# Seven-product pairs in the first output block of a hybrid decoder layer, their shared products between the last gate tiles

## The chip, the cores and the metric

One core of one Trainium2 chip. The metric is the device time of one launch in microseconds (us); the kernel before takes 1085.87 us (median of 3 runs, 1085.77 to 1085.95). Engine names are those of the profile: PE is the matrix engine (PEld its weight loads), DVE the vector engine, ACT the scalar engine, POOL the general engine, SP the engine whose queue issues the loads.

## The reference

One decoder layer on 256 tokens of width 2048, all in float32. What the change touches is the output projection of the mixed heads:

```python
u = rmsnorm(h, ln1_w)
lru_x, lru_g, q, k, v, ret_g = split(u @ w_in)          # six pieces, 1024 columns each
y_lru = rg_lru(conv(lru_x)) * gelu(lru_g)               # (256, 1024)
y_ret = silu(ret_g) * group_norm(retention(q, k, v))    # (256, 1024)
h = h + concat([y_lru, y_ret]) @ w_out                  # (2048, 2048): the change is here
u = rmsnorm(h, ln2_w)
h = h + (silu(u @ w_ffn_gate) * (u @ w_ffn_up)) @ w_ffn_down
return rmsnorm(h, final_norm_w)
```

## The kernel before

**Precision.** Each float32 operand is cut in two parts that the PE takes at its fast rate: a high part, cast by ACT (L112), and a rest, subtracted by DVE (L113). A product of two such operands is three matmuls: high by high, high by low, low by high (`three`, L667 to L672). So each weight that is loaded costs ACT one cast and DVE one subtraction before PE can use it. A load is 128 partitions by 1024 columns (512 KB) into one of six `raw` tiles; its parts lie in one of four `wh` and one of four `wl` tiles. The loads run three ahead of their use.

**The order of the work.** A list named `program` holds the steps; each step names the weights it needs and the function that issues its matmuls. First come the six input projections. The last of them is `lru_gate`: eight tiles of 128 columns (`fm_tile`, L173 to L189, tiles named `fm`), each with 16 matmuls of 512 columns and 16 of 256 and two loads. After each, `lru_out` (L411) makes one piece of the left operand `y`: a copy and an add out of the accumulator, a multiply, a gelu by a square and a tanh, and a multiply with the recurrence `hs`. Two pieces make a pair `y[k]`, cut by `Left` (L537). `y[0]` to `y[3]` come from these tiles, `y[4]` to `y[7]` from the retention heads: `group_norm` (L510) scales the head outputs `o` (eight ACT operations and two of DVE per four heads), then `ret_y` (L525) turns each head by two PE transposes into a tile `yt`.

**Blocks.** Then come two output blocks and eleven of the feed-forward part, then the down projection. A block is 1024 columns by eight pairs of row tiles; its four accumulators are c11, c12, c21 and c22 (two token halves by two column halves). `room(index)` (L663) puts them in one of two sets of four PSUM banks: the even blocks in the set that `aux` uses, the odd ones in the set that `bank` uses, where the `fm` tiles are too. A *plain* pair is eight products, 24 matmuls of 512 columns (`plain`, L793), from two loads. A *summed* pair takes seven products by sums of its tiles, in two steps. Its *shared* step (`share`, L771) makes four products, 12 matmuls, into the four accumulators before the block begins. After a block's last shared step DVE and ACT combine the accumulators (L781 to L787). The *direct* step (`direct`, L789) later adds the other three products, 9 matmuls. For the shared step DVE adds weight tiles four times (L648, in `raw`) and the parts are cut in four pieces; for the direct step half of the weights is loaded and cut again. The left operand of such a pair needs four small sums (s1 to s4, L551 to L554) and their cut.

`SUMMED` (L32) names the summed pairs of each block, `STEPS` (L36) the order of plain steps (p), direct steps (d) and shared steps of the next block (s), and `PLAIN` (L35) the order of the plain pairs. Block 0 has no summed pair and holds two shared steps of block 1; block 1 has pairs 4 and 5.

**Queues.** Each engine works through its own queue in order. The order in each queue is set when the program is built, by a scheduler that keeps to the program's order but may put a later instruction ahead where it takes an earlier one not to be ready. `defer` and `tick` (L228 to L241) put off the heads' work by a number of steps.

Of the kernel before, what the change touches and what calls it, by code (L numbers as in the profile page):

```python
# [17 lines left out]
KT = D // P  # L18
DFF = 5632
FT = DFF // P  # L20
NLRU = 8
# [7 lines left out]

SUMMED = ((), (4, 5), (2, 3)) + ((1, 2, 3), (0, 1, 2, 3)) * 4 + ((1, 2, 3), (1, 2, 3))  # L32
SUMMED_OUT, SUMMED_FFN = (4, 5), (0, 1, 2, 3)

PLAIN = ((4, 5, 6, 7, 0, 1, 2, 3),) * 2 + (tuple(range(8)),) * 11  # L35
STEPS = ("pppspppspp", "ppspdpsdpp", "pdpsdpspspp") + ("pspsdpsdpsdp", "psdpsdpsddp") * 4 + ("psdpsdpsdpp", "psdpsdpsdpp")  # L36


EARLY_DOWN = (0, 1, 2)
# [5 lines left out]
def tile_hymba_layer(ctx: ExitStack, tc: tile.TileContext, A: dict, out: bass.AP):  # L45
# [33 lines left out]
    def bank(name):  # L79
        return pmm.tile([P, 512], F32, tag="mm", name=nm(name))  # L80

    def aux(name):
        return paux.tile([P, 512], F32, tag="aux", name=nm(name))
# [65 lines left out]
    program = []  # L149
# [23 lines left out]
    def fm_tile(unit, acts, order, post, room=bank):  # L173


        def run():
            ps = room("fm")
            for n in range(0, len(order), 2):
                if n == 8 and halfway:
                    halfway.pop()()  # L180

                two = [(*unit.part(k, P, 0, P), acts[k]) for k in order[n : n + 2]]
                for i, (wh, _, hl) in enumerate(two):
                    pe.matmul(ps, wh, hl, start=n + i == 0, stop=False)  # L184
                for i, (_, wl, hl) in enumerate(two):
                    pe.matmul(ps[:, :S], wl, hl[:, :S], start=False, stop=n + i == len(order) - 1)  # L186
            post(ps)

        program.append(([unit], run))  # L189
# [94 lines left out]
    u = [None] * KT  # L284
# [126 lines left out]
    def lru_out(n, ps):  # L411
        g, q = tmp("g"), tmp("q")
        halves(ps, g)
        v.tensor_tensor(out=g, in0=g, in1=r1, op=ALU.mult)
        act.activation(out=q, in_=g, func=AF.Square, scale=math.sqrt(0.044715))
        v.scalar_tensor_tensor(out=q, in0=q, scalar=1.0, in1=g, op0=ALU.add, op1=ALU.mult)
        act.activation(out=q, in_=q, func=AF.Tanh, scale=math.sqrt(2.0 / math.pi))
        v.scalar_tensor_tensor(out=g, in0=q, scalar=1.0, in1=g, op0=ALU.add, op1=ALU.mult)
        v.scalar_tensor_tensor(
            out=y_half(n), in0=g, scalar=0.5, in1=pair(hs, n, "hs"), op0=ALU.mult, op1=ALU.mult  # L420
        )
        y_done(n)

        cb, t = divmod(n, 2)
        htok[cb, t] = res_tile("htok")
        nc.sync.dma_start(out=htok[cb, t], in_=A["x_tok"][t * P : t * P + P, cb * 512 : cb * 512 + 512])
# [96 lines left out]
            v.tensor_scalar(out=gnh, in0=small[:, C_GN : C_GN + NH], scalar1=0.5, scalar2=None, op0=ALU.mult)  # L523

    def ret_y(h):  # L525
        ps = aux("yt")
        for t in range(2):
            o = oo[2 * t + h // 4][:, (h % 4) * P : (h % 4) * P + P]
            pe.transpose(ps[:, t * P : t * P + P], o, ident)
        act.activation(out=y_half(NLRU + h), in_=ps[:, :S], func=AF.Copy, scale=gnh[:, h : h + 1])  # L530
        y_done(NLRU + h)
# [527 lines left out]
        tm_block([Unit(A["w_rg"][4 * c + i]) for i in range(4)], lambda k: u[k], post)  # L1059
    head_at = len(program) - 8  # L1060

    for n in range(NLRU):
        fm_tile(Unit(A["w_lg"][n]), u, range(KT), lambda ps, n=n: lru_out(n, ps))

    def swap():

        early.close()
# [5 lines left out]
        for j in range(NB)  # L1073
    ]
    down = Block(NB + 2, lambda i: A["w_down"][i], dl, None, "", EARLY_DOWN, make_left)
    for b, after in zip(blocks, blocks[1:] + [down]):
        if b.index == 2:
            program.append(([], swap))
        b.put(after)
        if b.index == NB:  # L1080
            program.append(([], load_fw))
# [120 lines left out]
```

## Time and profile before

| | |
|---|---|
| median of 3 runs | 1085.87 us |
| profiled execution, first to last instruction | 1084.4 us |
| PE busy | 1074.2 us (99%) |
| DVE busy | 953.5 us (88%) |
| ACT busy | 660.9 us (61%) |
| mean granted PE clock | 0.999 |
| loads of weights, each 512 KB | 3.4 to 6.3 us from issue to landing |

The last input projection runs from 243.8 to 291.7 us after the start of the span, block 0 follows it. The profile gives a time to every instruction of each engine's queue, and for an idle stretch the engine that ended it. PE and DVE instructions overlap their neighbours, so the cost of one in a full queue is the distance from its start to the next start, and not the duration that its row lists.

### The profile page before, as it was taken

What the parts mean: (1) busy time and instruction counts of PE and PEld (TensorE: products, weight loads), DVE (VectorE), ACT (ScalarE), POOL (GpSimd) and SP (SyncE); (2) the same over time, 40 slices, a digit from 0 to 9 for tenths busy, and PEclk for the clock granted to TensorE, in tenths of its full rate; (3) what the DMA queues carried; (4) which work ended last, traced back from release to release, by engine and by line L of the source; (5) the groups of instructions that cost most, each with busy time, mean ns of one, the idle gap of its engine ahead of it and who ended that gap; (6) DMA issues with size and microseconds to landing.
All of it is one profiled execution on the core that took longest, in us unless ns stands there. A gap on an engine that the chain in (4) does not pass through costs nothing.

```text
span 1084.4 us, 14584 instructions
## 1 busy us (share of the span) xinstructions
PE 1074.2 (99%) x5101; PEld 899.5 (83%) x5101; DVE 953.5 (88%) x1371; ACT 660.9 (61%) x935; POOL 51.0 (5%) x61
## 2 busy tenths in 40 slices
PE   9999999999999999999999999999999999999997
PEld 7888888888888788888888888888888888888885
DVE  7789799988878889888998998999899899898986
ACT  7666644468746676565566566556556666655563
POOL 0612230000000000000000000000000000000001
PEclk9999999999999999999999999999999999999999
DMA  9964474444565567577677677686675756465652
GB/s 330 333 211 168 160 252 173 174 175 171 181 230 205 184 228 275 198 248 266 220 245 261 220 264 235 233 289 214 233 271 194 265 181 213 171 214 199 212 209 85
DMA packets 69274, 238.32 MB, mean 220 GB/s; under 512 B 7888, under 2 KB 8272, under 8 KB 69200
## 3 DMA queue, kind: packets, MB, share of 16 engines
q1 hardware_dynamic: 68400, 235.29, 62.7%
q0 software_dynamic: 512, 1.57, 0.4%
q8 instruction: 40, 0.66, 0.2%
q10 hardware_dynamic: 288, 0.52, 0.1%
q14 instruction: 34, 0.28, 0.1%
HBM read 235.26 MB, written 2.10 MB: 219 GB/s over the span
## 4 chain that ended last, share of the span: by engine, by line
PE 97%; DVE 1%; issue 1%; DMA 0%; ACT 0%; POOL 0%; SPq 0%; POOLq 0%; ACTq 0%
PE c L670 22%; PE c L672 22%; PE c L671 22%; PE fm L184 11%; PE fm L186 5%; PE tm L164 3%; PE tm L165 3%; PE tm L166 3%; PE p L672 1%; PE p L671 1%; PE p L670 1%; PE ft L833 1%; DMA raw<-in_w_v 0%; PE ht L576 0%; PE sc L482 0%
## 5 line engine op out<-in xcount | busy, mean ns | idle before, releaser
L112 ACT CAST wh<-raw 128x1024 fp32r<-128x1024 f32 (+1 forms) x490 | 460.9, 965 | 362.6 <-PE c L672 132.5
L113 DVE TENSOR_TENSOR wl<-raw,wh 128x1024 fp32r<-128x1024 f32 (+1 forms) x490 | 538.2, 1122 | 91.2 <-ACT wh L112 88.4
L671 PE MATMUL c<-wl,ah 128*128 128x512 f32 x850 | 331.0, 390 | 0.0
L672 PE MATMUL c<-wh,al 128*128 128x512 f32 x850 | 330.4, 389 | 0.0
L670 PE MATMUL c<-wh,ah 128*128 128x512 f32 x850 | 275.0, 391 | 0.2 <-ACT wh L112 0.2
L670 PEld LDWEIGHTS c<-wh,ah 128*128 128x128 f32 x850 | 159.4, 188 | 33.4 <-ACT wh L112 1.1
L672 PEld LDWEIGHTS c<-wh,al 128*128 128x128 f32 x850 | 159.6, 188 | 33.0
L671 PEld LDWEIGHTS c<-wl,ah 128*128 128x128 f32 x850 | 159.6, 188 | 32.7
L184 PE MATMUL fm<-u,wh 128*128 128x512 f32 x512 | 161.3, 396 | 0.0
L186 PEld LDWEIGHTS fm<-u,wl 128*128 128x128 f32 x512 | 96.0, 188 | 22.5
L186 PE MATMUL fm<-u,wl 128*128 128x256 f32 x512 | 101.1, 278 | 0.0
L184 PEld LDWEIGHTS fm<-u,wh 128*128 128x128 f32 x512 | 78.4, 189 | 0.3
L648 DVE TENSOR_TENSOR raw<-raw,raw 128x512 f32<-128x512 f32 x106 | 73.1, 690 | 2.8
L648 DVE TENSOR_TENSOR raw<-raw 128x512 f32<-128x512 f32 x106 | 72.7, 689 | 2.4
L671 PE MATMUL c<-wl,sh 128*128 128x512 f32 x176 | 68.5, 389 | 0.0
L672 PE MATMUL c<-wh,sl 128*128 128x512 f32 x176 | 68.0, 389 | 0.0
L670 PE MATMUL c<-wh,sh 128*128 128x512 f32 x176 | 60.4, 394 | 0.3 <-ACT sh L112 0.3
L165 PE MATMUL tm<-wl,u 128*128 128x512 f32 x128 | 48.8, 394 | 0.0
L166 PE MATMUL tm<-wh,u 128*128 128x512 f32 x128 | 48.7, 390 | 0.0
L164 PE MATMUL tm<-wh,u 128*128 128x512 f32 x128 | 47.3, 398 | 0.8 <-ACT u L288 0.8
L954 POOL TENSOR_TENSOR htok<-htok,fw 128x512 f32<-128x512 f32 x2 | 2.5, 1273 | 895.9 <-ACT junk L947 895.9
L670 PEld LDWEIGHTS c<-wh,sh 128*128 128x128 f32 x176 | 33.1, 188 | 7.3 <-ACT sh L112 0.7
(245 smaller groups left out, 1034.9 us busy)
## 6 DMA issues: line engine op xcount, KB each, us to landing
raw<-in_w_gu SPq DMA_DIRECT2D x212, 512.0 KB, 5.5
raw<-in_w_down SPq DMA_DIRECT2D x91, 512.0 KB, 4.3
raw<-in_w_out SPq DMA_DIRECT2D x34, 512.0 KB, 3.7
raw<-in_w_lx SPq DMA_DIRECT2D x16, 512.0 KB, 6.3
raw<-in_w_k SPq DMA_DIRECT2D x16, 512.0 KB, 3.5
raw<-in_w_q SPq DMA_DIRECT2D x16, 512.0 KB, 4.0
raw<-in_w_rg SPq DMA_DIRECT2D x16, 512.0 KB, 3.4
raw<-in_w_lg SPq DMA_DIRECT2D x16, 512.0 KB, 3.4
```

The costliest lines, as they stand in the source:

```text
L112: act.copy(out=dst_h, in_=src)
L113: v.tensor_tensor(out=dst_l, in0=src, in1=dst_h.bitcast(F32), op=ALU.subtract)
L164: pe.matmul(ps, ah, wh, start=first, stop=False)
L165: pe.matmul(ps, ah, wl, start=False, stop=False)
L166: pe.matmul(ps, al, wh, start=False, stop=last)
L184: pe.matmul(ps, wh, hl, start=n + i == 0, stop=False)
L186: pe.matmul(ps[:, :S], wl, hl[:, :S], start=False, stop=n + i == len(order) - 1)
L648: v.tensor_tensor(out=dst, in0=a, in1=b, op=ALU.add)
L670: pe.matmul(p, ah, bh, start=first, stop=False, skip_group_check=onto)
L671: pe.matmul(p, ah, bl, start=False, stop=False, skip_group_check=onto)
L672: pe.matmul(p, al, bh, start=False, stop=last, skip_group_check=onto)
L833: pe.transpose(pt[:, o : o + P], g[:, (2 * b + c) * P : (2 * b + c) * P + P], ident)
```

## The change

Block 0 takes pairs 4 and 5 as summed pairs, and block 1 takes pair 6 besides 4 and 5. Pair 6 (heads 4 and 5) gets the sums of its left tiles. The two shared steps of block 0 are put into `program` behind gate tiles 3 and 5 (counted from 0). Since the accumulators of block 0 then hold all four banks of the `aux` set from the first shared step on, the transposes of `ret_y` go to the other set. Block 0 holds three shared steps of block 1. The line numbers of the new kernel are 2 higher than those of the old up to L1060.

```diff
-SUMMED = ((), (4, 5), (2, 3)) + ((1, 2, 3), (0, 1, 2, 3)) * 4 + ((1, 2, 3), (1, 2, 3))
-SUMMED_OUT, SUMMED_FFN = (4, 5), (0, 1, 2, 3)
+SUMMED = ((4, 5), (4, 5, 6), (2, 3)) + ((1, 2, 3), (0, 1, 2, 3)) * 4 + ((1, 2, 3), (1, 2, 3))
+SUMMED_OUT, SUMMED_FFN = (4, 5, 6), (0, 1, 2, 3)
+
+SHARED_FIRST = (3, 5)
...
-STEPS = ("pppspppspp", "ppspdpsdpp", "pdpsdpspspp") + ("pspsdpsdpsdp", "psdpsdpsddp") * 4 + ("psdpsdpsdpp", "psdpsdpsdpp")
+STEPS = ("pspdpspdpsp", "pdpspdpsdp", "pdpsdpspspp") + ("pspsdpsdpsdp", "psdpsdpsddp") * 4 + ("psdpsdpsdpp", "psdpsdpsdpp")
...
     def ret_y(h):
-        ps = aux("yt")
+        ps = bank("yt")
...
-    for n in range(NLRU):
-        fm_tile(Unit(A["w_lg"][n]), u, range(KT), lambda ps, n=n: lru_out(n, ps))
-
     def swap():
...
     down = Block(NB + 2, lambda i: A["w_down"][i], dl, None, "", EARLY_DOWN, make_left)
+
+    for n in range(NLRU):
+        fm_tile(Unit(A["w_lg"][n]), u, range(KT), lambda ps, n=n: lru_out(n, ps))
+        if n in SHARED_FIRST:
+            m = SHARED_FIRST.index(n)
+            program.append(([blocks[0].shared[m]], lambda m=m: blocks[0].share(m)))
+
```

**ACT's queue around the first gate tile.** sh_515 is the cut of the sums of `y[4]`; rg and sg are the retention gate and its tanh for the last four heads; yf_533 is `y[5]` out of its transposes, ah_535 its high part; the wh tiles are high parts of gate weights (wh_547 for the first half of gate tile 2), fm_549 is gate tile 0. Before:

```order
L112 CAST sh_515_2612<-s_514_2607 128x512
L473 ACTIVATE rg_528_2657<-tm_474_2414,r1_tok_108 128x512
L474 ACT_TABLE_LOAD
L474 ACTIVATE sg_529_2658<-rg_528_2657 128x512
L473 ACTIVATE rg_530_2674<-tm_475_2415,r1_tok_108 128x512
L112 CAST wh_557_2792<-raw_556_2791 128x1024
L170 COPY g_550_2758<-fm_549_2725 128x256
L474 ACTIVATE sg_531_2675<-rg_530_2674 128x512
L530 ACTIVATE yf_533_2682<-yt_532_2679,gnh_117 128x256
L530 ACTIVATE yf_533_2682<-yt_534_2684,gnh_117 128x256
L112 CAST wh_560_2798<-raw_559_2797 128x1024
L112 CAST ah_535_2688<-yf_533_2682 128x512
```

The same place in the changed kernel:

```order
L114 CAST sh_515_2612<-s_514_2607 128x512
L475 ACTIVATE rg_528_2657<-tm_474_2414,r1_tok_108 128x512
L476 ACT_TABLE_LOAD
L476 ACTIVATE sg_529_2658<-rg_528_2657 128x512
L475 ACTIVATE rg_530_2674<-tm_475_2415,r1_tok_108 128x512
L476 ACTIVATE sg_531_2675<-rg_530_2674 128x512
L532 ACTIVATE yf_533_2682<-yt_532_2679,gnh_117 128x256
L532 ACTIVATE yf_533_2682<-yt_534_2684,gnh_117 128x256
L114 CAST ah_535_2688<-yf_533_2682 128x512
L114 CAST wh_547_2720<-raw_546_2719 128x1024
L114 CAST sh_538_2697<-s_537_2692 128x512
L499 COPY o_483_2478<-pv_540_2701 128x128
```

The heads' work, up to the cut of `y[5]`, now stands ahead of the cut of gate weights: wh_547 comes behind it, where before wh_547 was long done and two later tiles (wh_557, wh_560) stood among the heads' rows.

**DVE's queue at the end of the gate tiles.** fm_641 is the last gate tile of the kernel before. Its rows there, and the first weights of block 1's first shared step (wl_662, raw_660):

```order
L171 TENSOR_TENSOR g_642_3219<-fm_641_3186,g_642_3219 128x256
L419 SCALAR_TENSOR_TENSOR yf_633_3170<-g_631_3161,hs_479_2451 128x256
L414 TENSOR_TENSOR g_642_3219<-g_642_3219,r1_109 128x256
L113 TENSOR_TENSOR wl_652_3244<-raw_650_3241,wh_651_3243 128x1024
L416 SCALAR_TENSOR_TENSOR q_643_3220<-q_643_3220,g_642_3219 128x256
L113 TENSOR_TENSOR wl_659_3278<-raw_657_3275,wh_658_3277 128x1024
L418 SCALAR_TENSOR_TENSOR g_642_3219<-q_643_3220,g_642_3219 128x256
L419 SCALAR_TENSOR_TENSOR yf_633_3170<-g_642_3219,hs_479_2451 128x256
L113 TENSOR_TENSOR wl_662_3284<-raw_660_3281,wh_661_3283 128x512
L113 TENSOR_TENSOR al_645_3230<-yf_633_3170,ah_644_3229 128x512
```

In the changed kernel c11_612, c12_615, c22_613 and c21_614 are block 0's accumulators; L785 to L789 combine them after its second shared step; raw_673, wl_675 and wl_666 belong to block 1's first shared step (wl_666 is written twice; this is its second half), fm's last values are g_668:

```order
L785 TENSOR_TENSOR p_648_3198<-c12_615_3040,p1_647_3197 128x512
L115 TENSOR_TENSOR wl_675_3334<-raw_664_3270,wh_674_3333 128x1024
L418 SCALAR_TENSOR_TENSOR q_669_3310<-q_669_3310,g_668_3309 128x256
L650 TENSOR_TENSOR raw_673_3325<-raw_673_3325 128x512
L786 TENSOR_TENSOR q_649_3199<-p_648_3198,c22_613_3032 128x512
L421 SCALAR_TENSOR_TENSOR yf_659_3260<-g_657_3251,hs_479_2451 128x256
L115 TENSOR_TENSOR wl_666_3273<-raw_673_3325,wh_665_3272 128x512
L420 SCALAR_TENSOR_TENSOR g_668_3309<-q_669_3310,g_668_3309 128x256
L788 TENSOR_TENSOR c22_613_3032<-q_649_3199,c21_614_3036 128x512
L789 TENSOR_TENSOR c21_614_3036<-c21_614_3036,p_648_3198 128x512
L115 TENSOR_TENSOR wl_680_3344<-raw_678_3341,wh_679_3343 128x1024
```

The shared step of block 1 and the combining of block 0's accumulators now stand among the last gate tiles' own rows; before, weights of plain pairs (wl_652, wl_659) stood there, and the first shared step began behind them.

**PE's queue where block 0 begins.** Before, the last gate tile (fm_641) is followed by block 0's first plain pair:

```order
L186 MATMUL fm_641_3186<-u_43_303,wl_626_3118 128x256
L670 MATMUL c11_653_3247<-wh_628_3124,ah_512_2603 128x512
L671 MATMUL c11_653_3247<-wl_629_3125,ah_512_2603 128x512
L672 MATMUL c11_653_3247<-wh_628_3124,al_513_2604 128x512
L670 MATMUL c12_654_3251<-wh_628_3124,ah_512_2603 128x512
L671 MATMUL c12_654_3251<-wl_629_3125,ah_512_2603 128x512
```

In the changed kernel block 1's first shared step (c11_687, c22_688, c21_689, c12_690) comes right behind the last gate tile, mixed with block 0's first plain pair (c11_612, c12_615). Here is the end of that step, 16 matmuls behind the last gate tile:

```order
L673 MATMUL c21_689_3391<-wl_675_3334,sh_515_2612 128x512
L674 MATMUL c21_689_3391<-wh_674_3333,sl_516_2613 128x512
L672 MATMUL c11_612_3028<-wh_679_3343,ah_604_3012 128x512
L673 MATMUL c12_690_3395<-wl_666_3273,sh_515_2612 128x512
L674 MATMUL c12_690_3395<-wh_665_3272,sl_516_2613 128x512
L672 MATMUL c12_615_3040<-wh_654_3214,ah_582_2919 128x512
```

The shared step of block 1 has moved up from behind three plain pairs to the very start of block 0.

## The prediction

> **What bounds the kernel now.** I read the page's busy times and chain first, then what PE waited for.
>
> ```profile
> PE 1074.2 (99%) x5101; PEld 899.5 (83%) x5101; DVE 953.5 (88%) x1371; ACT 660.9 (61%) x935; POOL 51.0 (5%) x61
> PE 97%; DVE 1%; issue 1%; DMA 0%; ACT 0%; POOL 0%; SPq 0%; POOLq 0%; ACTq 0%
> PE warm L105 <- DVE eps_t L98: 1.1, 1, 1.1
> PE tm L164 <- ACT u L288: 0.8, 2, 0.5
> PE c L670 <- ACT wh L112: 0.2, 1, 0.2
> ```
>
> PE is the bound, and its queue is nearly never empty: its waits add up to a few us, most of them at the start. A matmul taken out is worth its full slot, as long as PE stays fed. But DVE is at 88% on average, so the question is whether it can feed PE where the change puts its work: between the gate tiles. The windows view has DVE there, and at the end of block 0 and in block 1 (length, busy us, instructions):
>
> ```profile
> 245.10:294.25 49.15, 43.68 (x88) 1.00 0.49 176
> 364.00:391.00 27.00, 25.45 (x36) 1.00 0.67 242
> ```
>
> Along the gate tiles DVE has 5.47 us free in 49.15. It is also ahead of PE, but not by much: the rest of block 0's first weights is subtracted at 284.84 and done at 286.1, and PE takes it at 291.96, right behind the first row of block 0 (291.72). That lead, 5.9 us, is about what four split tiles allow: three lie ahead of the one in use.
>
> **The prices.** PE's timeline, for the slots:
>
> ```profile
> 243.78 0.62 PE L184 MATMUL fm<-u,wh 128*128 128x512 f32 x2
> 247.27 0.39 PE L491 MATMUL pv<-v,sc 128*128 128x128 f32 x2
> 247.94 0.60 PE L482 MATMUL sc<-rope,rope 128*128 128x256 f32 x2
> 248.59 0.60 PE L529 MATMUL yt<-ident,o 128*128 128x128 f32 x4
> 248.95 0.72 PE L184 MATMUL fm<-u,wh 128*128 128x512 f32 x2
> 291.72 0.40 PE L670 MATMUL c<-wh,ah 128*128 128x512 f32 x1
> 308.73 0.62 PE L670 MATMUL c<-wh,sh 128*128 128x512 f32 x2
> ```
>
> From 291.72 to 308.73 stand 75 matmuls of 512 columns: 0.227 each. The first gate tile makes ten matmuls of each size from 243.78 to 247.27, so a tile (16 of each) is 5.58. Three attention matmuls are 0.67, four transposes 0.36.
>
> DVE's timeline, for the distances between starts in a full queue:
>
> ```profile
> 258.00 0.28 DVE L551 TENSOR_TENSOR s<-yf 128x128 f32<-128x128 f32 x1
> 258.20 0.28 DVE L553 TENSOR_TENSOR s<-yf 128x128 f32<-128x128 f32 x1
> 258.40 0.48 DVE L499 BATCH_NORM_STATS2 st<-o 128x6 f32<-128x128 f32 x2
> 267.69 1.22 DVE L113 TENSOR_TENSOR wl<-raw,wh 128x1024 fp32r<-128x1024 f32 x1
> 268.82 0.16 DVE L255 TENSOR_TENSOR gr<-rs,rs 128x8 f32<-128x8 f32 x1
> 271.05 0.41 DVE L171 TENSOR_TENSOR g<-fm,g 128x256 f32<-128x256 f32 x1
> 271.39 0.41 DVE L418 SCALAR_TENSOR_TENSOR g<-q,g 128x256 f32<-128x256 f32 x1
> 284.84 1.22 DVE L113 TENSOR_TENSOR wl<-raw,wh 128x1024 fp32r<-128x1024 f32 x1
> 300.79 0.69 DVE L113 TENSOR_TENSOR wl<-raw,wh 128x512 fp32r<-128x512 f32 x1 [0.27 <-ACT wh L112]
> 301.40 0.68 DVE L113 TENSOR_TENSOR al<-yf,ah 128x512 fp32r<-128x512 f32 x1
> 302.00 0.68 DVE L648 TENSOR_TENSOR raw<-raw 128x512 f32<-128x512 f32 x1
> 302.72 1.42 DVE L648 TENSOR_TENSOR raw<-raw,raw 128x512 f32<-128x512 f32 x2
> 304.17 0.69 DVE L648 TENSOR_TENSOR raw<-raw 128x512 f32<-128x512 f32 x1
> 304.78 1.82 DVE L113 TENSOR_TENSOR wl<-raw,wh 128x1024 fp32r<-128x1024 f32 x2
> 306.52 0.68 DVE L113 TENSOR_TENSOR t4l<-raw,t4h 128x512 fp32r<-128x512 f32 x1
> 307.12 1.22 DVE L113 TENSOR_TENSOR wl<-raw,wh 128x1024 fp32r<-128x1024 f32 x1
> ```
>
> 1024 columns cost 1.14, 512 cost 0.61, 256 cost 0.34, a small sum 0.20, the four weight sums 2.78 (0.695 each). The last eight rows are one shared step: 0.61, 2.78, then 1.74 and 0.60, together 5.73, and a cut of left tiles (0.60) in between.
>
> **The change part by part.** *Removed.* Three pairs become summed ones, each three matmuls fewer: 9 × 0.227 = 2.04 us of PE. With a full queue that is 1085.87 − 2.04 = 1083.83. The profiled execution's span, 1084.4, is 1.5 below the median; I take that difference as unchanged.
>
> *Added to DVE.* A summed pair costs 5.73 for its shared and 1.14 for its direct step, where a plain pair costs 2 × 1.14: 4.6 more, 13.8 for three. The sums of `y[6]` add 4 × 0.20 + 0.61 = 1.4, the combining of block 0 another 4 × 0.61 = 2.4. So DVE gets 17.6 us more while PE gets shorter.
>
> *Where it lands.* Two shared steps go between the gate tiles, and by DVE's queue the first one of block 1 lies there too, and the combining. I count DVE's queue of the changed kernel from the cut of `y[4]`'s left tile to the second half of wl_666, for which the 18th matmul behind the last gate tile waits: 120 instructions, of which 18 × 1.14 = 20.5, 24 × 0.61 = 14.6, 38 × 0.34 = 12.9, 12 weight sums × 0.695 = 8.3, 12 small sums × 0.20 = 2.4, 16 short ones (statistics at 0.20, the rest down to 0.08, one of 384 columns) 2.1: 61.0 us. The same prices over the 88 instructions of the quoted window give 42.6 where the window has 43.68, so the count is, if anything, 2.5% low.
>
> DVE can begin when `y[4]` is out and cast. ACT's timeline:
>
> ```profile
> 243.07 0.84 ACT L530 ACTIVATE yf<-yt,gnh 128x256 f32<-128x256 f32 x2 [0.44 <-PE yt L529]
> 244.98 0.62 ACT L112 CAST ah<-yf 128x512 fp32r<-128x512 f32 x1
> 249.61 0.68 ACT L473 ACTIVATE rg<-tm,r_tok 128x512 f32<-128x512 f32 x1
> 250.31 1.28 ACT L474 ACT_TABLE_LOAD   x1
> 251.60 0.63 ACT L474 ACTIVATE sg<-rg 128x512 f32<-128x512 f32 x1
> 261.20 1.28 ACT L248 ACT_TABLE_LOAD   x1
> 270.07 3.18 ACT L520 ACTIVATE o<-o,gm,gr 128x128 f32<-128x128 f32 x8
> ```
>
> The cast now follows yf at once: 243.07 + 0.84 + 0.62 = 244.5. DVE is through at 244.5 + 61.0 = 305.5 if it never waits.
>
> PE's side: the attention and transposes that stood inside the first gate tile (247.27 to 248.95) now stand ahead of it, so the tile starts at 243.78 + 1.68 = 245.46. To the matmul in question stand 8 tiles (44.6), 24 + 17 matmuls of 512 columns (the two shared steps, and what precedes it behind the last gate tile), 9.3, eight transposes 0.7 and three attention matmuls 0.7: 55.3 us, so PE is there at 300.8. It waits at least 305.5 − 300.8 = 4.7.
>
> *DVE's own waits.* By ACT's new order the heads' work stands first. Walking both queues with these durations, DVE waits 0.5 for the cast of `y[4]`'s sums, 1.25 and 0.5 for the two sg behind the table load, 0.6 for `y[5]`'s cast, 0.45 around two more table loads, and 0.55 and 0.95 for the eight o's (3.18 on ACT): 4.8. From the first shared step on ACT has less to do than DVE, and DVE has no more waits. The bounds are 0 and the 5.5 that DVE had free in the quoted window; I take 4.8, since each of these waits has its row. PE's wait: 4.7 + 4.8 = 9.5. It shows in pieces: 1.6 at the transposes ahead of gate tile 3 (they need o, done on DVE at 264.5 by the walk; PE is there at 245.46 + 3 × 5.58 + 0.67 = 262.9), 2.6 in the first shared step, the rest in block 1's first shared step.
>
> *After that.* Block 0 has three shared, two direct and six plain steps: 12 + 9 matmuls three and two times and 24 six times, 198 × 0.227 = 44.9 on PE, against 3 × 5.73 + 2 × 1.14 + 12 × 1.14 = 33.2 of cuts and sums on DVE and some 7 beside. DVE gets its lead back there. In block 1 I count by the same prices 39.4 on DVE against 40.1 on PE over the shared steps of block 2; a lead of up to 5.9 covers that. Cost: 0; with no lead, PE waits once for a cast and a cut, the cut 1.14 and the cast about the same, 2.3.
>
> *At nothing.* Three more loads of 512 KB: SP issues them three loads ahead, and the six raw tiles cover their landing. Without that cover one is a few us. The other bank set for `ret_y`: gate tile 3 takes over the bank of gate tile 1, whose values DVE has read by 262.6, before PE asks at 262.9; 0 to 0.5.
>
> Sum: 1085.87 − 2.04 + 9.5 = 1093.3 us.
>
> **The clock.** The first matmuls of the run, after PE had nothing real to do, are slow; the third row is the settled rate:
>
> ```profile
> 4.93 1.22 PE L164 MATMUL tm<-wh,u 128*128 128x512 f32 x2
> 5.95 0.82 PE L165 MATMUL tm<-wl,u 128*128 128x512 f32 x2
> 6.61 0.63 PE L166 MATMUL tm<-wh,u 128*128 128x512 f32 x2
> ```
>
> The two slow rows lose 0.78 us against the third. [...] No row of the kernel before shows a fall in mid-kernel, since PE has no gap there. [...]
>
> **The rivals.** *PE stays full* (the other side): DVE's free 5.47 us and its 5.9 us lead take up the added work, and the nine matmuls are gain. Place: the 18th matmul of block 0. It decides if DVE's 61.0 plus waits come to less than 300.8 − 244.5 = 56.3. For it: PE never waited before at DVE loads as high as 25.45 in 27. Against: even with no wait the count is 4.7 too long. 1083.83.
>
> *Only one wait counts*: the transposes' 1.6 us are paid, and in that time DVE catches up for good. 1085.87 − 2.04 + 1.6 = 1085.4. Against it: DVE's total does not shrink while PE waits.
>
> *The clock falls* in the gaps, at three places: 3 × 0.78 = 2.3 more, 1095.6. For it: gaps of 2 us and more close together.
>
> *The lead is gone in block 1* as well, where DVE and PE are level by my count: PE waits again for a cast and a cut, 2.3, 1095.6; with the 2.5% by which my count may be low (1.5 us) 1097.1. For it: DVE's 25.45 in 27 before the change. Against: block 0 has room for the lead to come back.
>
> **How the numbers follow.** Chances: the forecast 0.66, PE stays full 0.08, only one wait 0.06, the clock 0.12, the lead 0.08. Around the forecast the bounds of DVE's waits give 1088.6 (none) to 1094.0 (5.5). The range is 1086.5 to 1097.5: below, the first bound less 2 us for a count 3% high; above, the last rival and a little. It leaves out the first two rivals and a twentieth above. 0.2% is 2.2 us, about what a measurement of this kernel can tell from no change. A full PE queue gains 2.04, just inside it, so faster by over 0.2% needs that rival and a little more: 0.03. Within 0.2% (1083.7 to 1088.0): 0.11. Slower: 0.86.
>
> **What would show it.** Right: DVE without idle stretches from the first shared step to block 0; PE waiting for DVE or ACT at yt, at c22 and c12 of the shared steps, about 9 us in all between 262 and 315; the last gate tile ending at about 291.7 + 5.4 + 4.2 = 301.3. Wrong: waits of PE under 4 us there; DVE with idle time between gate tiles 4 and 7; new PE waits in later blocks, which my counts deny; a granted clock under 1 in this stretch.

## The result, and the profile after

The changed kernel takes 1096.26 us (median of 4 runs, 1093.96 to 1098.16) against 1085.91 us (4 runs, 1085.77 to 1086.44) of the kernel before on the same chip: ratio of the means 1.0094, 95% interval 1.0082 to 1.0106, so 10.2 us slower (the medians lie 10.35 apart). The profiled execution took 1095.59 us, its span is 1093.7 us against 1084.4: 9.3 more.

Busy times and the chain of the changed kernel:

```profile
PE 1075.3 (98%) x5092; PEld 898.3 (82%) x5092; DVE 967.4 (88%) x1401; ACT 667.5 (61%) x947; POOL 50.9 (5%) x61
PE 94%; DVE 2%; ACT 1%; issue 1%; DMA 1%; POOL 0%; SPq 0%; POOLq 0%; ACTq 0%; DVEq 0%
```

PE has its nine matmuls less and yet more busy time: in part by its clock (below), and in part because a row of 0.39 us, which lies under its neighbour after 0.23 in a full queue, counts whole in front of a gap. DVE and ACT now hold 3% of the chain together. What PE waited for:

```profile
PE fm L186 <- ACT rg L475: 2.8, 1, 2.8
PE c L672 <- ACT wh L114: 2.4, 4, 1.2
PE c L673 <- DVE wl L115: 2.0, 2, 1.4
PE c L672 <- ACT p L784: 1.4, 1, 1.4
```

None of these is in the profile of before, but for 0.2 us. The first is in front of the first gate tile. PE's timeline there:

```profile
245.45 0.38 PE L485 MATMUL sc<-rope,rope 128*128 128x128 f32 x2
248.68 1.22 PE L186 MATMUL fm<-u,wh 128*128 128x512 f32 x2 [2.85 <-ACT rg L475]
...
252.21 0.63 PE L186 MATMUL fm<-u,wh 128*128 128x512 f32 x2
...
252.91 0.63 PE L186 MATMUL fm<-u,wh 128*128 128x512 f32 x2
```

From 245.45 to 248.68 PE does 0.11 us of work: a gap of 3.12 us. The four banks of the `bank` set then hold the two tiles of the retention gate (`tm`) and the two tiles of transposes (`yt`) that the change has put there, and the gate tile waits until ACT has copied a `tm` out. ACT's rows say why that is late: the copy stands behind a cut that waits for DVE.

```profile
247.43 0.62 ACT L114 CAST sh<-s 128x512 fp32r<-128x512 f32 x1 [1.77 <-DVE s L556]
247.95 0.68 ACT L475 ACTIVATE rg<-tm,r_tok 128x512 f32<-128x512 f32 x1
```

Behind the gap the matmuls are slow. Three sets of four take 3.53 us from 248.68 to 252.21, where the set from 252.21 to 252.91 takes 0.70: 1.43 us lost. The windows view (length, then busy us of PE, PEld, DVE, ACT, POOL, then the granted clock):

```profile
245.00:248.40 3.40, 0.83 (x6) 0.59 (x4) 2.88 (x11) 1.63 (x5) 0.00 (x0) 0.97 0.49 175
248.40:251.80 3.40, 3.12 (x10) 2.69 (x11) 1.53 (x3) 3.34 (x6) 0.00 (x0) 0.53 0.20 80
251.80:255.20 3.40, 3.40 (x23) 3.07 (x22) 2.63 (x7) 2.63 (x6) 0.00 (x0) 1.00 0.00 0
```

The clock is halved for 3.4 us. In these 3.4 us, where PE is late already, DVE is busy for only 1.53 us: it waits for ACT as well, so it gains little on PE.

The later waits, PE's rows in the first shared step and behind the last gate tile:

```profile
277.67 0.50 PE L673 MATMUL c<-wl,sh 128*128 128x512 f32 x1 [1.41 <-DVE wl L115]
...
303.95 0.39 PE L674 MATMUL c<-wh,al 128*128 128x512 f32 x1
...
305.72 0.50 PE L672 MATMUL c<-wh,ah 128*128 128x512 f32 x1 [1.38 <-ACT p L784]
...
309.16 0.50 PE L673 MATMUL c<-wl,sh 128*128 128x512 f32 x1 [0.58 <-DVE wl L115]
...
311.53 0.50 PE L672 MATMUL c<-wh,ah 128*128 128x512 f32 x1 [1.18 <-ACT wh L114]
311.87 0.40 PE L673 MATMUL c<-wl,sh 128*128 128x512 f32 x1
```

By the distances between starts PE loses 1.57 us in the first shared step and 4.15 in four gaps from 303.95 to 311.53. The last of these four ends with ACT's cast of a plain pair's weights, which by the profile had itself waited for PE:

```profile
310.43 1.04 ACT L114 CAST wh<-raw 128x1024 fp32r<-128x1024 f32 x1 [0.54 <-PE c L674]
```

A last gap of 0.90 us stands in block 1, at 385. The sum: 3.12 + 1.43 + 1.57 + 4.15 + 0.90 = 11.17, less 2.04 for the nine matmuls, is 9.13 of the 9.3 us.

DVE, at the place where the prediction's ledger ends (the second half of wl_666):

```profile
310.86 0.72 DVE L115 TENSOR_TENSOR wl<-raw,wh 128x512 fp32r<-128x512 f32 x1
```

It is done 0.60 later, at 311.5; the ledger with DVE's own waits said 310.3. So DVE's queue ends when the cast above does, and the 18th matmul could not have gone earlier than 311.5 without that cast either. From 270 to 312 us DVE has no idle time. From 244.4, the cut of `y[4]`, to 311.5 it waits for 6.4 us and works for 60.7.

### The profile page after: what moved, and what is told of

It reads as the page before. It is cut to its first block, busy times and chain, and to the rows that moved or that the text cites. A ratio compares the mean times of both kernels' runs of the same rounds, so it can differ in the third digit from the quotient of the medians.

```text
span 1093.7 us, 14622 instructions
## 1 busy us (share of the span) xinstructions
PE 1075.3 (98%) x5092; PEld 898.3 (82%) x5092; DVE 967.4 (88%) x1401; ACT 667.5 (61%) x947; POOL 50.9 (5%) x61
## 3 DMA queue, kind: packets, MB, share of 16 engines
q0 software_dynamic: 512, 1.57, 0.4%
## 4 chain that ended last, share of the span: by engine, by line
PE 94%; DVE 2%; ACT 1%; issue 1%; DMA 1%; POOL 0%; SPq 0%; POOLq 0%; ACTq 0%; DVEq 0%
PE c L673 22%; PE c L674 22%; PE c L672 22%; PE fm L186 10%; PE fm L188 5%; PE tm L166 3%; PE tm L167 3%; PE tm L168 3%; PE p L674 1%; PE p L673 1%; PE p L672 1%; PE ft L835 1%; DMA x<-in_x 1%; DVE wl L115 0%; ACT wh L114 0%
## 5 line engine op out<-in xcount | busy, mean ns | idle before, releaser
L673 PE MATMUL c<-wl,ah 128*128 128x512 f32 x832 | 324.0, 390 | 0.0
L674 PE MATMUL c<-wh,al 128*128 128x512 f32 x832 | 323.4, 389 | 0.0
L672 PE MATMUL c<-wh,ah 128*128 128x512 f32 x832 | 268.0, 391 | 3.5 <-ACT wh L114 2.1
L672 PEld LDWEIGHTS c<-wh,ah 128*128 128x128 f32 x832 | 155.9, 188 | 37.1 <-ACT wh L114 3.9
L186 PE MATMUL fm<-u,wh 128*128 128x512 f32 x512 | 162.1, 398 | 2.8 <-ACT rg L475 2.8
L186 PEld LDWEIGHTS fm<-u,wh 128*128 128x128 f32 x512 | 79.0, 190 | 3.4 <-ACT rg L475 3.0
L650 DVE TENSOR_TENSOR raw<-raw,raw 128x512 f32<-128x512 f32 x112 | 77.5, 692 | 2.7
L650 DVE TENSOR_TENSOR raw<-raw 128x512 f32<-128x512 f32 x112 | 77.0, 691 | 2.4
L673 PE MATMUL c<-wl,sh 128*128 128x512 f32 x188 | 73.4, 390 | 2.0 <-DVE wl L115 2.0
L674 PE MATMUL c<-wh,sl 128*128 128x512 f32 x188 | 72.7, 389 | 0.0
L672 PE MATMUL c<-wh,sh 128*128 128x512 f32 x188 | 64.8, 394 | 0.2 <-ACT wh L114 0.2
L673 PEld LDWEIGHTS c<-wl,sh 128*128 128x128 f32 x188 | 35.3, 188 | 10.0 <-DVE wl L115 2.7
```

The costliest lines, as they stand in the source:

```text
L650: v.tensor_tensor(out=dst, in0=a, in1=b, op=ALU.add)
L672: pe.matmul(p, ah, bh, start=first, stop=False, skip_group_check=onto)
L673: pe.matmul(p, ah, bl, start=False, stop=False, skip_group_check=onto)
L674: pe.matmul(p, al, bh, start=False, stop=last, skip_group_check=onto)
```

## The experiments

Two theories stood at the start. *Theory 1*, the prediction's: the length of DVE's queue sets when PE can go on behind the gate tiles, and an early wait of PE only takes the place of a later one. *Theory 2*: the early gap of 3.12 us and the half clock behind it, which the prediction had put at nothing, are a loss of their own. All ratios are of means, to the kernel before, which had medians of 1085.8 to 1086.0 us beside the experiments. Each experiment has four to six runs where no number is given.

**1. The transposes of the first four heads on the old bank set.**

```diff
-        ps = bank("yt")
+        ps = (bank if h >= 4 else aux)("yt")
```

> The changed kernel with one part undone: the transposes of the first four heads (those that make `y[4]` and `y[5]`) take their tiles from the old bank set again, so that the first gate tile need not wait for ACT to copy the retention gate out of its bank. The accumulators of block 0 are not yet held at that point. Theory 1 (DVE's queue between the gate tiles sets when block 0 can begin, and an early wait of PE only takes the place of a later one): DVE has the same instructions; what it gains is at most the 1 to 1.5 us by which ACT's old order lets it wait less. 1094.8 to 1096.3 us, the 3.0 us gap in front of the first gate tile gone and the waits at the first shared step and behind the last gate tile longer by about as much. Theory 2 (the bank wait of 3.0 us and the clock that falls behind it, 1.4 us, are a loss of their own): 4.4 less, 1091.9 us.

Measured: 1097.77 us, ratio 1.0108 (1.0094 to 1.0122), 1.5 us above the range of theory 1 and 5.9 above the number of theory 2. The early gap is gone, and PE waits in the first shared step and at the transposes of the other heads:

```profile
PE c L672 <- ACT wh L114: 4.8, 5, 3.2
PE yt L531 <- DVE o L523: 2.6, 1, 2.6
```

By the starts these are gaps of 3.37 us at 264.5 and 2.78 at 272.2, with the clock at 0.50 from 269.9 to 273.3 and again from 276.8 to 280.2. That looks like theory 1, but the edit does more than take the early gap out. It undoes the new bank set for half of the transposes only, and those of the other heads now make PE wait in front of gate tile 3 (experiments 8 to 10). And PE's queue now has the first shared step behind gate tile 2: its first product starts at 264.0, where in the changed kernel it starts at 273.7, behind gate tile 3. There its sums and casts are not ready. So this run does not decide between theories 1 and 2.

**2. Block 1's first shared step two steps later.**

```diff
-STEPS = ("pspdpspdpsp", ...
+STEPS = ("ppdpsdpspsp", ...
```

> The changed kernel with block 1's first shared step two steps later: block 0 begins with two plain pairs (24 matmuls for 2.28 us of DVE) and not with one plain pair and a shared step (12 matmuls for 5.73 us). Theory 1: DVE has one shared step less, 5.7 us and a cut of 0.6, to do before PE needs its result; the waits behind the last gate tile, 4.2 us together, go, and block 0 with 44.9 us of PE against some 40 of DVE takes the step up: 1091.5 to 1092.5 us, with the 3.0 us in front of the first gate tile still there. Rival 3 (DVE's total is the limit, wherever the step stands): the waits come back inside block 0, 1095.5 to 1096.5 us. Theory 2 alone says nothing of this step; by it the early 4.4 us remain, so no less than 1091 us.

Measured: 1098.49 us, ratio 1.0117 (1.0102 to 1.0133), above even the range of rival 3, and not by its mechanism. The waits did not come back inside block 0: they became one wait at its start. PE's row, and ACT's rows around the copy that it waited for:

```profile
306.36 0.80 PE L672 MATMUL c<-wh,ah 128*128 128x512 f32 x1 [4.26 <-ACT p L784]
```

```profile
304.90 0.62 ACT L114 CAST ah<-yf 128x512 fp32r<-128x512 f32 x1 [1.05 <-DVE yf L421]
305.42 0.41 ACT L419 ACTIVATE q<-q 128x256 f32<-128x256 f32 x1
305.74 0.57 ACT L784 COPY p<-c 128x512 f32<-128x512 f32 x1
```

The copy of c11 opens the combining of block 0, and block 0's first plain product goes into c11. Its last shared product was made at 288.5, so it could have been copied 17 us earlier; in ACT's queue it stands behind the cut of `y[2]`, which waits for DVE. So there may be a third cause, the place of the combining in the queue (*theory 5*, which experiment 5 tests). The gap is 4.43 us, and the windows view has the clock halved for 6.8 us behind it:

```profile
301.80:305.20 3.40, 0.30 (x3) 0.10 (x1) 2.36 (x6) 1.92 (x4) 0.00 (x0) 1.00 1.01 401
305.20:308.60 3.40, 2.24 (x5) 1.82 (x6) 3.37 (x8) 1.95 (x6) 0.00 (x0) 0.50 0.67 240
308.60:312.00 3.40, 3.40 (x9) 2.64 (x8) 2.72 (x6) 1.10 (x2) 0.00 (x0) 0.50 0.06 11
```

**3. The third pair alone.** Block 0 without summed pairs, block 1 with three.

```diff
-SUMMED = ((4, 5), (4, 5, 6), ...
+SUMMED = ((), (4, 5, 6), ...
-SHARED_FIRST = (3, 5)
+SHARED_FIRST = ()
-STEPS = ("pspdpspdpsp", ...
+STEPS = ("ppsppspppsp", ...
-        ps = bank("yt")
+        ps = aux("yt")
```

> The third pair alone: block 1 takes pairs 4, 5 and 6 as summed pairs, with block 0 as in the kernel before (no summed pair, no shared step between the gate tiles, the transposes on the old bank set). Three matmuls less, 3 x 0.227 = 0.68 us; DVE gets 4.6 us for the pair and 1.4 for the sums of `y[6]`, spread over 50 us of block 0. Theory 1 (only the stretch between the gate tiles is too full): PE stays full, 1085.2 us. Rival (DVE's load in block 0 and 1 is at its limit too): one wait of about 0.9 us as it stands in block 1 of the changed kernel, 1086.1 us or more.

Measured: 1088.08 us (11 runs), ratio 1.0019 (1.0010 to 1.0028): the rival's number, by another wait than the one it names. Block 1 now begins before its three shared steps are combined:

```profile
PE c L672 <- ACT c L787: 1.5, 1, 1.5
```

L787 is the other copy of a combining, and the gap is 1.7 us. Against the 0.68 us that the three matmuls save, that is 1.0 of the 2.1 us; the rest has no one place in the profile. So this pair is a small loss by itself, at the edge of what can be told.

**4. Block 0's weight sums on POOL.**

```diff
-                v.tensor_tensor(out=dst, in0=a, in1=b, op=ALU.add)
+                e.tensor_tensor(out=dst, in0=a, in1=b, op=ALU.add)
...
+            if index == 0:
+                for s in self.shared:
+                    s.adder = pool
```

> The changed kernel with the eight weight sums of block 0's two shared steps on POOL instead of DVE. DVE has 8 x 0.695 = 5.6 us less to do between the gate tiles. Theory 1: its queue ends 5 us earlier and PE's waits behind the last gate tile (4.2 us) go: 1091.5 to 1092.5 us. Rival 4 (what counts is the chain of the first shared step, load, sums, cast, cut, not DVE's total): POOL's sums take longer one by one and stand four in a row, so PE waits longer in the two shared steps and nothing is won, 1095 us or more. Theory 2: the early 4.4 us stay, the rest may go.

Measured: 1098.81 us, ratio 1.0116 (1.0103 to 1.0130). That is rival 4's number, but it says nothing against theory 1, since DVE got no time back (`e` is `adder`). POOL's rows in the first shared step, and DVE's beside them:

```profile
267.96 1.41 POOL L650 TENSOR_TENSOR raw<-raw 128x512 f32<-128x512 f32 x1 [93.65 <-DVE wl L115]
269.44 2.78 POOL L650 TENSOR_TENSOR raw<-raw,raw 128x512 f32<-128x512 f32 x2
272.30 1.34 POOL L650 TENSOR_TENSOR raw<-raw 128x512 f32<-128x512 f32 x1
```

```profile
268.59 1.07 DVE L416 TENSOR_TENSOR g<-g,r 128x256 f32<-128x256 f32 x1
269.58 1.50 DVE L420 SCALAR_TENSOR_TENSOR g<-q,g 128x256 f32<-128x256 f32 x1
271.11 1.40 DVE L421 SCALAR_TENSOR_TENSOR yf<-g,hs 128x256 f32<-128x256 f32 x1
272.43 1.50 DVE L418 SCALAR_TENSOR_TENSOR q<-q,g 128x256 f32<-128x256 f32 x1
273.85 0.68 DVE L115 TENSOR_TENSOR al<-yf,ah 128x512 fp32r<-128x512 f32 x1
```

DVE's four operations, 0.34 each elsewhere, take 5.26 us from 268.59 to 273.85: 3.9 us lost while POOL works. The second step costs as much again (from 286.52 to 292.47, 5.95 us for 1.90 of work). DVE lost 8 us and was spared 5.6.

**5. Experiment 2, with the second shared step behind gate tile 4.**

```diff
-SHARED_FIRST = (3, 5)
+SHARED_FIRST = (3, 4)
```

> The kernel of the run before with block 1's first shared step two steps later, and besides block 0's second shared step behind gate tile 4 instead of 5. In that earlier run PE stood 4.3 us behind the last gate tile for ACT's copy of c11, which had been ready since 290 us and was made at 305.7: in ACT's queue it stood behind the cut of `y[2]` (pair of gate tiles 4 and 5), which DVE reached late. With the step one tile earlier the copy stands seven places earlier in ACT's queue, ahead of that cut. Theory 5 (the place of the combining in the queue, and the half clock behind the gap of 4.4 us, took back what the later step had won): gap and fall go, 4.4 + 2.6 us; up to 3 us of new waits in the second shared step, which DVE must feed 5.6 us earlier: 1091.5 to 1094.5 us. Theory 1 in its strict form (only the length of DVE's queue counts): the same rows of DVE, so the same end, 1097.5 to 1099 us.

Measured: 1092.54 us, ratio 1.0063 (1.0049 to 1.0076), as theory 5 has it. PE no longer waits behind the last gate tile. What it waited for most:

```profile
PE fm L186 <- ACT rg L475: 2.8, 1, 2.8
```

The gap in front of the first gate tile is 3.12 us again, and here the clock stays at 1.00 behind it. DVE has the same operations as in experiment 2: the 6 us, with the 6.8 us of half clock among their causes, come from the order alone.

**6. One summed pair in block 0, its shared step behind gate tile 3.** The first four heads' transposes are on the old set, as in experiment 1.

```diff
-SUMMED = ((4, 5), (4, 5, 6), ...
-SUMMED_OUT, SUMMED_FFN = (4, 5, 6), (0, 1, 2, 3)
-SHARED_FIRST = (3, 5)
-STEPS = ("pspdpspdpsp", "pdpspdpsdp", ...
+SUMMED = ((4,), (4, 5), ...
+SUMMED_OUT, SUMMED_FFN = (4, 5), (0, 1, 2, 3)
+SHARED_FIRST = (3,)
+STEPS = ("pppspdpspp", "ppspdpsdpp", ...
```

> One summed pair in block 0 (pair 4) with its shared step behind gate tile 3; blocks 1 and on as in the kernel before, the transposes of the first four heads on the old bank set. DVE gets 4.6 us for the pair and 2.4 us for the combining, 7.0 in all, against the 5.5 us free and the 5.9 us of lead that the profile of before has there. PE has three matmuls less. Theory 1: it fits, PE stays full, 1085.9 - 0.7 = 1085.2 us. Rival 6 (any shared step between the gate tiles costs PE the chain of sums, cast and cut, some 3 us, whatever room DVE has, and perhaps a fall of the clock): 1088 to 1091 us.

Measured: 1096.12 us, ratio 1.0090 (1.0077 to 1.0104). With 7.0 of the 17.6 us of added work it costs as much as the whole change, so theory 1 in the form of a sum over the whole stretch falls: DVE is idle for 4.0 of the 6 us from 276 to 282. PE waits at the same two places as in experiment 1:

```profile
262.29 0.40 PE L672 MATMUL c<-wh,ah 128*128 128x512 f32 x1
...
266.36 1.72 PE L672 MATMUL c<-wh,sh 128*128 128x512 f32 x3 [3.22 <-ACT wh L114]
...
273.71 0.69 PE L531 MATMUL yt<-ident,o 128*128 128x128 f32 x2 [2.60 <-DVE o L523]
```

The first row is the first product of the shared step. As in experiment 1 it stands behind gate tile 2 in PE's queue, one tile ahead of its place in `program`. The granted clock is 0.50 from 265.2 to 278.9 us. By the distances between starts the waits are 6.5 us and the slow matmuls about 4.7 more, so the clock is a large part of the price of this order.

**7. The changed kernel without block 0's weight sums.** What is multiplied there are the weights as loaded.

```diff
-            self.add(r)
+            if self.sums:
+                self.add(r)
...
+            if index == 0:
+                for s in self.shared:
+                    s.sums = False
```

> The changed kernel without the eight weight sums of block 0's two shared steps; the weights are cut as they are loaded, so block 0's result is another one. DVE has 8 x 0.695 = 5.6 us less, and no other engine gets it. Theory 1: the waits at the first shared step (1.4 us) and behind the last gate tile (4.2 us) go, the 3.0 us in front of the first gate tile stay: 1090 to 1091.5 us. Theory 2 (banks and clock alone) and rival 4 (the moved sums were no relief because the chain inside the step counts): no more than 2 us less, 1094 us or more.

Measured: 1090.77 us, ratio 1.0045 (1.0031 to 1.0059): 5.5 us less than the changed kernel, for 5.6 us less on DVE. The gaps in the first shared step and behind the last gate tile are gone, the early one stays (with half clock behind it), and one of 1.8 us at 278 is new. So DVE's load is a cause, at about its full price; the runs of each of the two kernels spread over 3.4 and 4.2 us. The sums also stand in the chain of the first shared step, so the gap there can't tell load from chain. Behind the last gate tile it can: block 1's shared step keeps its sums, and nothing waits for it. The order changes with the load, though: that step now stands behind 27 of block 0's own matmuls.

**8. Experiment 6, with the shared step behind gate tile 5.**

```diff
-SHARED_FIRST = (3,)
+SHARED_FIRST = (5,)
```

> The kernel of the run before with one summed pair in block 0, its shared step behind gate tile 5 instead of 3; nothing else differs. With the step behind tile 3 PE stood 3.4 and 1.1 us in the step and 3.0 us at the transposes behind it, and the granted clock was 0.50 for some 12 us. Theory 7 (the place decides: up to gate tile 4 DVE is in arrears with the heads' cuts, sums and scalings, from tile 5 on it has room, and by then the two o's are done): no wait of over 1 us and no fall of the clock, 1085 to 1086.5 us, a drop of 10 us for the same work. Theory 1 as first put (one ledger over the whole stretch, in which early and late work count alike) would have had the run before at 1085.2 and gives the same here, so it can't explain a difference. Rival 6 (a shared step between the gate tiles costs its chain of sums, cast and cut wherever it stands): 1090 us or more.

Measured: 1096.31 us, ratio 1.0096 (1.0081 to 1.0111). Theory 7 falls, and so does rival 6, since the step itself does not wait. PE stands at one place:

```profile
262.76 0.39 PE L188 MATMUL fm<-u,wl 128*128 128x256 f32 x2
271.08 0.69 PE L531 MATMUL yt<-ident,o 128*128 128x128 f32 x2 [7.94 <-DVE o L523]
```

The first transposes of the last four heads stand in front of gate tile 3 in PE's queue. In the kernel before, o is done no earlier (its last row on DVE starts at 273.28, here at 271.88), but all these transposes stand inside gate tile 5, at 276.4 and 277.3, and nobody waits. So the new bank set may have moved them: it is the set of the gate tiles, and with it a transpose keeps its place among these, ahead of the next gate tile (*theory 8*).

**9. Both pairs of block 0, shared steps behind gate tiles 5 and 6.** The first four heads' transposes are on the old set.

```diff
-SUMMED = ((4, 5), (4, 5, 6), ...
-SUMMED_OUT, SUMMED_FFN = (4, 5, 6), (0, 1, 2, 3)
-SHARED_FIRST = (3, 5)
-STEPS = ("pspdpspdpsp", "pdpspdpsdp", ...
+SUMMED = ((4, 5), (4, 5), ...
+SUMMED_OUT, SUMMED_FFN = (4, 5), (0, 1, 2, 3)
+SHARED_FIRST = (5, 6)
+STEPS = ("ppdpsdppsp", "ppspdpsdpp", ...
```

> Both summed pairs in block 0, shared steps behind gate tiles 5 and 6, the first four heads' transposes on the old bank set, block 1 with pairs 4 and 5 only and its shared steps where the kernel before has them. Six matmuls less than before, 1.36 us. DVE gets 9.2 us for the pairs and 2.4 us for the combining, and has some 2 us free behind gate tile 4, and 5.9 us of lead. Theory 7: no wait in front of the first step, no fall; the second step and the start of block 0 wait for DVE by 11.6 - 7.9 = 3.7 us, less what block 0's plain pairs give back: 1085 to 1088.5 us. Rival 5 (the combining stands behind the cut of `y[2]` in ACT's queue, so that block 0 starts late, and the clock falls in that gap): 1090 to 1095 us.

Measured: 1099.98 us, ratio 1.0132 (1.0115 to 1.0149). That is above both ranges. The same gap of 8.1 us, and then rival 5's as well:

```profile
PE yt L531 <- DVE o L523: 7.9, 1, 7.9
PE c L672 <- ACT p L784: 2.5, 1, 2.5
```

**10. Three kernels, each with that one line undone for all heads.**

```diff
-        ps = bank("yt")
+        ps = aux("yt")
```

In experiment 8's kernel:

> One line differs from the earlier kernel with one summed pair behind gate tile 5: all transposes of `ret_y` take their tiles from the old bank set, as in the kernel before. There PE stood 8.1 us in front of gate tile 3, at the transposes of `y[6]`, for the two o's; with the transposes in the bank set of the gate tiles they keep their place among these, while in the old set they may stand behind gate tile 4, where the kernel before has them. Theory 8 (the bank set couples the transposes to the gate tiles, and PE waits in order for what DVE and ACT make late): the 8.1 us and the fall of the clock behind them go, 1085 to 1087 us. Rival 6 (a shared step between the gate tiles costs its chain wherever it stands): 3 us in the step, 1089 us or more.

In the changed kernel:

> The changed kernel with the one line of `ret_y` undone for all eight heads. Block 0's accumulators then wait for the last transposes to leave the banks, so the first shared step stands in the middle of gate tile 5's place instead of behind tile 3, and the second follows it at once. DVE's rows are the same as in the changed kernel. Theory 8: no wait in front of the first gate tile (3.0 us, and the 1.4 us of slow clock), none at the transposes; what is left is DVE's queue behind: 1089 to 1092.5 us. Theory 1 in its strict form (the end of DVE's queue counts, 61 us of work and its own waits, so the early waits come back behind the last gate tile): 1094 to 1097.5 us.

In experiment 9's kernel:

> One line differs from the earlier kernel with both summed pairs of block 0 behind gate tiles 5 and 6: all transposes of `ret_y` on the old bank set. Theory 8: the 8.1 us in front of gate tile 3 and the half clock behind them (some 1.8 us) go, the 2.7 us behind the last gate tile (the copy of c11, behind the cut of `y[2]` in ACT's queue) stay or grow, since PE comes 8 us earlier to the place and DVE does not: 1088 to 1091 us. Theory 1 in its strict form (11.6 us more work for DVE against 11.4 us of room): 1084.5 to 1086 us. Rival (the early wait was only the form in which DVE's lateness showed): 1096 us or more.

| | new set (for some or all heads) | old set | ratio of the latter |
|---|---|---|---|
| one pair, behind tile 5 | 1096.31 | 1089.51 | 1.0033 (1.0021 to 1.0044) |
| the changed kernel | 1096.26 | 1091.07 | 1.0042 (1.0029 to 1.0054) |
| two pairs, behind tiles 5 and 6 | 1099.98 | 1089.90 | 1.0035 (1.0023 to 1.0047) |

The waits that theory 8 names go all three times, and with them 6.8, 5.2 and 10.1 us for one line. In none of the three does PE wait in front of the first gate tile or at the transposes, which stand inside gate tile 5 or right in front of it. With one pair, and with two pairs behind tiles 5 and 6, the shared steps keep their places, so the moved transposes alone are tested there. In the changed kernel the first shared step moves too, from behind gate tile 3 (273.7) into gate tile 5 (280.6).

What is left is told by the profiles. One pair: theory 8's number was 2.5 us too low. It is rival 6's number, but the step itself does not wait. The copy of c11 came late again, with a gap of 2.69 us and half a clock behind it:

```profile
294.80:298.20 3.40, 1.07 (x5) 0.89 (x6) 2.67 (x5) 2.69 (x6) 0.00 (x0) 1.00 0.99 353
298.20:301.60 3.40, 3.40 (x10) 2.65 (x9) 3.40 (x8) 1.42 (x3) 0.00 (x0) 0.51 0.53 186
```

The changed kernel with the old set: PE's waits, all for what DVE and ACT make of weights and heads:

```profile
PE c L672 <- ACT wh L114: 2.2, 3, 1.2
PE fm L188 <- DVE wl L115: 2.0, 3, 1.5
PE c L672 <- ACT yf L532: 0.9, 1, 0.9
```

By the starts, gaps of 1.67, 0.58, 1.40, 1.18 and 0.32 between 268 and 292 us: 5.15, with 0.89 in block 1. Nothing waits behind the last gate tile. Yet the second half of wl_666 is done at 310.1 there, only 1.4 us earlier than in the changed kernel. Its order differs: the combining begins on DVE at 300.6 instead of 307.3, so block 0's plain products can go first, and the matmul that needs this half is the 39th behind the last gate tile and not the 18th.

Two pairs: the second shared step makes PE wait in three gaps of 1.18, 0.50 and 0.55 us, and the clock falls there too:

```profile
289.20:292.60 3.40, 1.89 (x7) 0.66 (x5) 3.38 (x8) 3.40 (x6) 0.00 (x0) 1.00 0.31 117
292.60:296.00 3.40, 3.40 (x9) 2.79 (x10) 3.40 (x5) 2.74 (x5) 0.00 (x0) 0.50 0.62 199
```

None of the thirteen versions is faster than the kernel before. The nearest are the third pair alone (1.0019) and the three with the old bank set.

## Why the prediction was right, and where it was not

The forecast was 1093.3 us, slower by 7.4; measured is 1096.26, slower by 10.2. The direction and the stretch were right. The working was right in part, and that the sum came so near is in part luck: 4.55 us came at a place that had no entry, and the places that had one gave 5.72 for 9.5.

- **Removed, 2.04 us.** Right: 5092 matmuls for 5101, and the sum of gaps above closes with it.
- **Added to DVE.** Right where it could be tested: the weight sums, 5.6 us by the quoted rows, gave 5.5 us of time when left out. The page's busy time rose by 13.9 us for the 17.6 forecast; in a fuller queue more of each row lies under its neighbour (the rows' durations add up to 24.4 us more).
- **The ledger.** DVE's end at 310.3 was measured as 311.5, and the gaps and slow matmuls up to there are 10.3 us for the 9.5 forecast. The work is 60.7 us for 61.0 (its terms add up to 60.9), DVE's own waits 6.4 for 4.8, over the bound of 5.5: a wait of 1.03 for a cast of gate weights, at 263, had no entry. In the order that the changed kernel has, the ledger gave the end to 1.2 us.
- **Where PE waits.** Half wrong. The 1.6 us at the transposes in front of gate tile 3 did not come; 3.12 us in front of the first gate tile did, with 1.43 of slow clock. In the first shared step it was 1.57 for 2.6; behind the last gate tile 4.15 for 5.3, of which 1.54 was a wait for the copy of c11, which the prediction never looked at: it counted the combining as work for DVE and not as something PE waits for. Of the signs that it named, DVE's full queue came; between 262 and 315 us PE waited 5.7 us and not about 9, and the last gate tile ended at 303.5 and not at 301.3.
- **"At nothing: the other bank set for `ret_y`, 0 to 0.5."** This step failed. Undoing that line alone, which also moves the first shared step, takes 5.2 us off. The prediction looked at the bank of gate tile 3, not at who holds the four banks when the first gate tile begins. The new order of ACT, which it did walk through (4.8 us of DVE's own waits), is an effect of the same line, but it was booked as a matter of DVE.
- **"DVE's total does not shrink while PE waits."** True, and yet the early wait was no advance on the late ones: with the early gap PE lost 4.55 us ahead and 5.72 later; with the old bank set none ahead and 5.15 later. DVE's end moved by 1.4 us; PE's order moved more. How much of the 5.2 us is the banks themselves, and how much the order that the scheduler makes of them, can't be told apart, since the one comes with the other.
- **After that, 0 to 2.3 us.** 0.90 in block 1; the third pair alone has a gap of 1.7 near there, for a copy of the combining and not for a cast.
- **The clock.** The sum went without a fall; the profiled execution has one, of 1.43 us, at a place that had no entry. The gap of 2.6 us that the prediction expected could have had one by itself: 2.10 us of idle PE had half clock behind them in experiment 9 (last section). Three falls were not there, and the rival's 0.78 us a fall, taken from the first rows of the run, was about half of the 1.43. The four runs go with the mean granted clock: 1093.96 us at 0.998, 1095.59 at 0.996, 1096.92 at 0.994, 1098.16 at 0.993.

Of the rivals, *PE stays full* and *only one wait counts* are out. *The clock falls* is right in kind, at one place rather than three. *The lead gone in block 1* shows as one wait of 0.90.

What stays open: why the scheduler puts the copy of c11 behind the cut of `y[2]`. That moving it pays, together with its shared step, is shown by experiment 5. How much of the 10.2 us each cause has can't be added up, since each edit that takes one away changes the order for the others.

## What to carry to other kernels

A line that only says from which pool a tile comes can cost as much as the work that the change adds: ask who holds the banks at the first moment of the new order, and which instructions now stand ahead of others in the queue of the engine that is the bound. A ledger of one engine's work gives the right end only for one order; look at what the bounding engine could do in the meantime, since that decided 5 us here at nearly the same end of DVE. Count every copy between two uses of an accumulator as a wait of PE, with its place in its engine's queue.

## What the runs showed of the hardware

**In these traces the granted clock changed in pieces of 3.4 us, and it was halved behind the pieces in which PE had been idle for 2.10 us or more.** The falls and rises of the granted clock lie whole multiples of 3.413 us apart: in the changed kernel at 248.21, at 251.62 (one piece on) and, when the work ends, at 1087.89 (246 pieces on); in the kernel before, the rise at 6.37 and the fall at the end, at 1081.57, are 315 pieces apart. So they lie on a grid, and the grid lies otherwise in each of the five executions below. The same gap of 3.12 us at the same instruction falls on it like this (in experiments 4 and 5 the grid is counted back from the fall at the end):

| profile | the piece with most of the gap ends at | PE idle in it, us | clock behind it |
|---|---|---|---|
| the changed kernel | 248.21 | 2.54 | half |
| experiment 7 | 247.94 | 2.26 | half |
| experiment 4 | 247.48 | 1.98 | full |
| experiment 2 | 247.20 | 1.76 | full |
| experiment 5 | 250.29 | 1.71 | full |

Idle time is counted here by the distances between starts. Between 15 and 1070 us of the fourteen traces, each piece at full clock with 2.10 us of idle PE or more has half clock behind it, and each with 1.99 or less has not. So a gap of 2.69 us had it (2.37 in one piece), and so had three gaps of 2.23 us together (2.22), where the windows view has PE busy for 1.89 of 3.40 us. Half clock lasted one piece, or two (behind the gap of 3.12 in experiment 7 and those of 4.43 and 8.1), or four (experiment 6), and cost 1.43 us where it was worked out for one. What sets the pieces, and what the limit between 1.99 and 2.10 us, no run shows.

**POOL and DVE held each other up in experiment 4.** Four DVE operations that start 0.34 us apart elsewhere took 1.07 to 1.50 us while POOL added tiles: they start 1.3 to 1.5 us apart from 269.58 to 273.85, beside sums of POOL that take 1.34 to 1.41 each. POOL's first sum in the second step took 2.35 us, most of it beside DVE operations at their usual distances, where the same sum took 1.41 in the first. What the two contend for, no run shows.

**PE took cut parts faster than uncut operands.** In the kernel before, one product of 256 columns on uncut float32 operands (`sc`, L482, two matmuls in the profile) takes 0.43 us from 247.94 to the next start; two products of 256 columns on cut parts (`fm`, L186, one matmul each) take 0.24 from 247.03.
